# The inverse of an RWKV-7 chunk applied, transposed, to the increment's rows and the outputs' block instead of to the keys and the values

## The chip, the cores and the metric

One core of a Trainium2 chip. Five engines run their own queues: TensorE (PE, matrix products; its weight loads are listed apart as PEld), VectorE (DVE), ScalarE (ACT), GpSimd (POOL) and SyncE (SP, which here issues the DMA transfers). The metric is the device time of one execution in microseconds (us); lower is better. The kernel before took 3070.48 us, the median of three runs (3066.96 to 3072.09).

## The reference, cut to what matters

The kernel is one decoder block over 2048 positions of 1024 channels: normalise, one wide input projection, a convolution branch and an RWKV-7 branch, two output projections, a merge, a last projection, a residual and a norm. The change touches the RWKV-7 state alone:

```python
def _rwkv7_scan(r, decay, k, v, kk, b):
    def step(state, inp):
        r_t, w_t, k_t, v_t, kk_t, b_t = inp
        sk = jnp.einsum('bhvk,bhk->bhv', state, kk_t)
        state = (state * w_t[:, :, None, :] - sk[..., None] * b_t[:, :, None, :]
                 + v_t[..., None] * k_t[:, :, None, :])
        return state, jnp.einsum('bhvk,bhk->bhv', state, r_t)
```

There are 16 heads of 64 channels, and everything is fp32.

## The kernel before, in words

**Blocks, groups, chunks.** The sequence is cut into 4 blocks of 512 positions. In each block the 16 heads make 4 groups of 4 heads (2 pairs `q` of 2 heads `hh`), so there are 16 groups in all. In a group the scan runs over `NCH` = 8 chunks of 64 positions. Within a chunk the recurrence is a triangular system of 64 x 64 for each head; it is inverted ahead, and the state `S` is carried from chunk to chunk. Even chunks (`e` = 0) and odd chunks (`e` = 1) keep their blocks in opposite halves of the 128 partitions: `vrow(e)` is the lower half for `e` = 0 and the upper for `e` = 1, and `prow(e)` the other half.

**Preparation** (`pair`, L718). For each pair it makes scaled keys and receptances `KR`, scaled increments' keys `BK`, their masked products `As` (`aux<-KR,BK`), the transposed rows `tk` of `BK`, the decay `pe`, and the values' rows `uv`.

**The inverse** (`group`, L861). The 32 x 32 diagonal quarters of each triangular block go out by DMA, are inverted on POOL in a loop of 31 steps (`TT`, `itmp`), and come back into `As` (`As<-dT`).

**The prelude** (from L917). The rest of the inverse and its use are products on TensorE. `turns(lower)`: 32 products 32 x 32 for the off-diagonal quarter, with `T11`, the transposed upper diagonal quarter that DVE makes, into the banks `late` and `aux`; DVE copies them to `Qs`. `rows64(xv, values)`: 32 products 64 x 64 that apply the value block of `As` to `uv`, into two `xo` banks. `turns(upper)`: 32 products 32 x 32 that finish the quarter, copied back into `As`. Then the keys in `KR` are transposed (`pk`, 16 products, `xo<-ident,KR`), copied by ACT to `Kt`, multiplied by the inverse (`pw`, 32 products 64 x 64) and copied back to `KR`; and the inverse is applied to `uv` (`xu`, 32 products 64 x 64, copied back by DVE and ACT).

**The chunk loop** (L1022). For each chunk: the product of `KR` with the state (`xo<-S,KR`), `uv` plus it (DVE), the increment `tk` times `uv` into columns 2 and 3 of the chunk's `xo` bank, and four DVE operations that bring `S` forward from these columns (`S<-xo,pe,Se`). After each odd chunk the outputs of the two chunks are made: 8 products of `As` with `uv` into columns 0 and 1 of both `xo` banks (`xo<-uv,As`, 128 partitions, 64 columns), then copied by ACT.

**What sets the order.** Everything up to the last projections is written out in a planner's order: tasks are Python generators that yield the time from which they can go on; `note` (L85) books each instruction on its engine with a cost from a table and moves the planner's clock by TensorE's work; `poll` takes the tasks that are due. Between the steps of a group's chain the planner puts products of the input projection, three by three (`ps_main`, 128 x 128 by 512 columns). Each engine then runs its queue strictly in that order, and waits on semaphores. An fp32 product smaller than the whole array stands as two MATMUL records in the trace.

**Side work** (`sides`, L1316) runs beside it: the next block's norm, the convolution's layer norm of the block before (`lnorm_first`), and `presplit`, which splits the weights of the last projections into a high and a low part ahead of their use.

Of the kernel before, what the change touches and what calls it, by code (L numbers as in the profile page):

```python
# [9 lines left out]
F32 = mybir.dt.float32  # L10
# [8 lines left out]
P = 128  # L19
# [4 lines left out]
CH = 64  # L24
# [47 lines left out]
def hybrid_block(ctx: ExitStack, tc: tile.TileContext, x, vecs, convk, w2a2, final_g, ada, w_in, w_co, w_ro, w_o, crow, out,  # L72
# [12 lines left out]
    def note(name, op, out, ins):  # L85
# [9 lines left out]
        if name == "PE":  # L95
            if op == "transpose":
                part, c = False, 0.218
            else:
                K_, M_, N_ = ins[0].shape[0], size(ins[0]), size(ins[1])
                part = K_ <= 64 or M_ <= 64  # L100
                c = N_ / 600 * ((0.27 if K_ <= 64 else 0.54) if M_ <= 64 else 0.89 if part else 1.0)
                if ins[1].dtype == F32R:
                    part, c = False, 0.015 + N_ / 2400
            if part != kind[0]:
                kind[0], c = part, c + (0.1 if part else 0.24)
            now[0] = t + c
            end = now[0] + 0.2
            joined[0] = True
        elif name == "SP":
            vt["SP"] = t + 0.36  # L110
            vt["DMA"] = max(vt["DMA"], t) + size(out) * out.shape[0] * 4 / DMA_RATE
            end = vt["DMA"] + 1.9
        else:
            c0, c1_ = RATE[name] if op != "memset" else (0.1, 0.9e-3)
            end = vt[name] = t + c0 + c1_ * max([size(out)] + [size(a) for a in ins[:1]])
# [745 lines left out]
    def group(G, before):  # L861
# [52 lines left out]
        yield when(lambda: G.pairs == 2 and (before is None or before.chained))  # L914
        yield ok(*As)

        T11 = lt.tile([P, 2, 2, NCH // 2, 32], F32, name="T11", tag="i2")  # L917
        Qs = lt.tile([P, 2, 2, NCH // 2, 32], F32, name="Qs", tag="i2")

        def quarters(e):  # L920
            p0 = 64 - 64 * e
# [1 line left out]

        every = [(q, hh, c) for q in range(2) for hh in range(2) for c in range(NCH // 2)]

        for e in (1, 0):
            lo_, hi_ = quarters(e)
            for q in range(2):
                nc.vector.transpose(heads(T11[:, q])[lo_], heads(As[q])[lo_, e::2, lo_])
        yield both(ok(T11, uv), free, bank("late"), bank("aux", 2), bank("xo", 2))  # L930
        locked[0] = True
        chains[0] += 1
        pq = [p_.tile([P, 2, 2, NCH // 2, 32], F32, name=n_, tag=n_) for p_, n_ in ((pl, "late"), (pa, "aux"))]

        def turns(mul):
            for n, (q, hh, c) in enumerate(every[::-1]):
                for e in range(2):
                    mul(e, q, hh, c, dict(start=(n == 0), stop=(n == 15), skip_group_check=True))

        def lower(e, q, hh, c, kw):  # L940
            lo_, hi_ = quarters(e)
            nc.tensor.matmul(pq[e][hi_, q, hh, c, :], As[q][lo_, hh, 2 * c + e, hi_], T11[lo_, q, hh, c, :], **kw)

        def upper(e, q, hh, c, kw):
            lo_, hi_ = quarters(e)
            nc.tensor.matmul(pq[e][lo_, q, hh, c, :], Qs[hi_, q, hh, c, :], As[q][hi_, hh, 2 * c + e, hi_], **kw)

        O = uv[:, 0::2]
        Sg = S[g]

        def two():
            return [px.tile([P, 2, 2, P], F32, name="xo", tag="xo") for _ in range(2)]

        def rows64(bank_, mul):
            for turn in range(2):
                for cl in range(2):
                    for q in range(2):
                        for hh in range(2):
                            for e in range(2):
                                n_ = turn ^ e  # L960
                                mul(e, 2 * n_ + cl, q, hh, bank_[n_][prow(e), cl, q, 64 * hh:64 * hh + 64],
                                    dict(start=(cl + q + hh == 0), stop=(cl + q + hh == 3), skip_group_check=True))

        def keep64(bank_, half):
            for e in range(2):
                (nc.scalar.copy if e else nc.vector.tensor_copy)(uv[prow(e), 4 * half + e:4 * half + 4:2], bank_[half][prow(e)])

        def values(e, cc, q, hh, dst, kw):
            vr, c, hs = vrow(e), 2 * cc + e, slice(64 * hh, 64 * hh + 64)
            nc.tensor.matmul(dst, As[q][vr, hh, c, kcol(e)], uv[vr, c, q, hs], **kw)  # L970

        def solved(e, cc, q, hh, dst, kw):
            pr_, c, hs = prow(e), 2 * cc + e, slice(64 * hh, 64 * hh + 64)
            nc.tensor.matmul(dst, As[q][pr_, hh, c, kcol(e)], uv[pr_, c, q, hs], **kw)

        turns(lower)
        with tc.high_priority(HP):
            for e in (1, 0):
                lo_, hi_ = quarters(e)
                nc.vector.tensor_copy(Qs[hi_], pq[e][hi_])  # L980
        xv = two()
        rows64(xv, values)
        for half in range(2):
            keep64(xv, half)
        yield ok(Qs, uv)

        turns(upper)
        with tc.high_priority(HP):
            for e in range(2):
                lo_, hi_ = quarters(e)  # L990
                for q in range(2):
                    nc.vector.tensor_copy(As[q][lo_, :, e::2, hi_], pq[e][lo_, q])
        Kt = lt.tile([P, 2, NCH // 2, P], F32, name="Kt", tag="La", bufs=1)
        pk = [px.tile([P, NCH // 2, P], F32, name="xo", tag="xo") for _ in range(2)]
        for q in range(2):
            for cc in range(NCH // 2):
                for e in range(2):
                    nc.tensor.matmul(pk[q][prow(e), cc, :], R[q]["KR"][:, cc, CH * (1 + e):CH * (2 + e)], ident,
                                     start=(cc == 0), stop=(cc == NCH // 2 - 1), skip_group_check=True)
            nc.scalar.copy(Kt[:, q], pk[q])  # L1000
        yield ok(Kt, *As)

        pw = [p_.tile([P, 2, NCH // 2, CH], F32, name=n_, tag=n_) for p_, n_ in ((pl, "late"), (pa, "aux"))]
        for n, (q, hh, cc) in enumerate(every):
            hs = slice(64 * hh, 64 * hh + 64)
            for e in range(2):
                nc.tensor.matmul(pw[e][hs, q, cc, :], Kt[prow(e), q, cc, hs], As[q][prow(e), hh, 2 * cc + e, kcol(e)],
                                 start=(q + cc == 0), stop=(q == 1 and cc == NCH // 2 - 1), skip_group_check=True)
        with tc.high_priority(HP):
            for q in range(2):  # L1010
                for e in range(2):
                    nc.scalar.copy(R[q]["KR"][:, :, CH * (1 + e):CH * (2 + e)], pw[e][:, q])
        xu = two()
        rows64(xu, solved)
        for half in range(2):
            keep64(xu, half)
        locked[0] = False
        yield ok(uv, R[0]["KR"], R[1]["KR"])

        xo = [px.tile([P, 4, P], F32, name="xo", tag="xo") for _ in range(2)]  # L1020
        every = [(q, hh, slice(64 * hh, 64 * hh + 64)) for q in range(2) for hh in range(2)]
        for c in range(NCH):  # L1022
# [12 lines left out]
            if e == 0:  # L1035
                for q in range(2):
                    nc.tensor.matmul(b_[:, 2 + q, :], R[q]["tk"][:, c, :], uv[:, c, q, :], start=False, stop=(q == 1),
                                     skip_group_check=True)
            else:
                for q, hh, hs in every:  # L1040
                    nc.tensor.matmul(b_[hs, 2 + q, 0:64], R[q]["tk"][:, c, hs], uv[:, c, q, hs], start=False,
                                     stop=(q + hh == 2), skip_group_check=True)
            with tc.high_priority(HP):
                for q, hh, hs in every:
                    nc.vector.scalar_tensor_tensor(out=Sg[hs, q, hs], in0=b_[hs, 2 + q, slice(0, 64) if e else hs],
                                                   scalar=R[q]["pe"][hs, c:c + 1], in1=Se[hs, q, hs],
                                                   op0=ALU.mult, op1=ALU.add)
            if e:
                for n, (q, hh, hs) in enumerate(every):
                    for i in range(2):  # L1050
                        nc.tensor.matmul(xo[i][vrow(i), q, hs], As[q][:, hh, c - 1 + i, rcol(i)], uv[:, c - 1 + i, q, hs],
                                         start=False, stop=(n == 3), skip_group_check=True)
                with tc.high_priority(HP):
                    for i in range(2):
                        nc.scalar.copy(O[vrow(i), cc], xo[i][vrow(i), 0:2])
# [183 lines left out]
        hx.give(mean, rl)  # L1239

    def lora_split(ps, out_):
        yield hx.room(3)
        lf, ll, lx = hx.take("lora"), hx.take("lora_lo"), hx.take("lora_x")
        yield from shifted(ps, T_LORA, lambda: lf)
        Task(lora_parts(lf, ll, lx, out_), 0)

    def lora_parts(lf, ll, lx, out_):
        yield ok(lf)
        nc.scalar.activation(lf[0:64], lf[0:64], AF.Tanh)
        lw = e1.tile([P, TB], F32R, name="lw", tag="lw")  # L1250
        la = e1.tile([P, TB], F32R, name="la", tag="la")
# [64 lines left out]
    def sides(b, g):  # L1316
# [3 lines left out]
                normed[0] = b + 1  # L1320
        if b == 1 and g == 0:
            yield from gate_col()
        if b and g == 2:
            yield from lnorm_first(b - 1)
        if b in (1, 2):
            for _ in range((2, 2, 0, 4)[g]):
                n_ = later.pop(0)
                for half in range(2):
                    yield from presplit(*n_, half)
# [358 lines left out]
```

## Time and profile before

| | |
|---|---|
| median of three runs | 3070.48 us |
| the profiled execution | 3068.1 us |
| its span, first to last instruction | 3066.4 us |
| instructions | 53344 |
| TensorE busy | 2807.9 us |
| VectorE busy | 2029.4 us |
| ScalarE busy | 1111.8 us |
| GpSimd busy | 1264.2 us |
| mean granted TensorE clock | 0.979 |

A row of the groups' view names the line, the engine and the operation, the tile written and the tiles read, the shape as rows*columns of the array and what is streamed through, the count, then the busy time and the mean of one, and the idle time of the engine just before with what ended it. All instructions have the line of the recording helper, L129, so they are told apart by their tiles. A row of the timeline gives the start, the time from the first start to the last end, and how many like instructions were merged in it. Matmuls overlap in the array and their ends are modelled, so what one costs is read from starts: the start of the next minus its own.

### The profile page before, as it was taken

How to read it: one execution, taken by the hardware profiler on the slowest of the kernel's cores; microseconds unless marked ns; L12 is line 12 of the kernel's file. 1: busy time of each engine (PE TensorE's matmuls, PEld its weight loads, DVE VectorE, ACT ScalarE, POOL GpSimd, SP SyncE). 2: the span in 40 equal slices, each digit the busy share in tenths (PEclk: the TensorE clock that was granted, in tenths of full speed). 3: DMA queues.
4: the chain of work that ended last, by engine and by line, in shares of the span. 5: the costliest groups of instructions: out<-in, count | busy, mean ns of one | idle time of the engine just before them, and what ended most of it. 6: DMA issues, size and time to landing. Idle time of an engine off the chain costs nothing.

```text
span 3066.4 us, 53344 instructions
## 1 busy us (share of the span) xinstructions
PE 2807.9 (92%) x19984; PEld 2287.7 (75%) x19984; DVE 2029.4 (66%) x3525; ACT 1111.8 (36%) x2232; POOL 1264.2 (41%) x1762
## 2 busy tenths in 40 slices
PE   5999989999999999899999998999999988899998
PEld 4777777777777777677777776787777776788988
DVE  6786777877575868584767676757486846643433
ACT  4544444443243333433433344333333323321211
POOL 2564645442535555335347554354554614200000
PEclk9999999999999999999999998999999998899999
DMA  8775767766767667577567564775565856776665
GB/s 296 251 275 204 262 211 249 252 210 215 228 201 235 210 194 247 182 242 225 196 228 254 175 232 152 237 243 193 189 207 169 274 168 239 265 232 229 206 226 176
DMA packets 361746, 680.53 MB, mean 222 GB/s; under 512 B 134160, under 2 KB 152912, under 8 KB 361488
## 3 DMA queue, kind: packets, MB, share of 16 engines
q1 hardware_dynamic: 361488, 677.13, 66.0%
q8 instruction: 157, 2.57, 0.3%
q14 instruction: 101, 0.83, 0.1%
HBM read 494.34 MB, written 181.54 MB: 220 GB/s over the span
## 4 chain that ended last, share of the span: by engine, by line
PE 39%; DVE 9%; POOL 8%; DMA 7%; issue 3%; SPq 1%; ACT 1%; DVEq 0%; POOLq 0%; ACTq 0%
PE ps_main L129 25%; PE xo L129 5%; PE pout L129 5%; POOL TT L129 2%; PE aux L129 2%; POOL itmp L129 2%; DVE acc L129 2%; DVE S L129 2%; PE late L129 2%; SPq L129 1%; POOL lny L129 1%; DMA dn<-dN 1%; DMA zb<-bv_d 1%; POOL oc L129 1%; DMA w_st<-w_ro_t 1%
## 5 line engine op out<-in xcount | busy, mean ns | idle before, releaser
L129 PE MATMUL ps_main<-h_hi,w_hi 128*128 128x512 f32 x2432 | 1017.4, 418 | 24.0 <-ACT w_hi L129 9.4
L129 PE MATMUL ps_main<-h_hi,w_lo 128*128 128x512 f32 x2432 | 965.7, 397 | 11.7 <-DVE w_lo L129 5.0
L129 PE MATMUL ps_main<-h_lo,w_hi 128*128 128x512 f32 x2432 | 962.3, 396 | 1.0 <-DVE h_lo L129 1.0
L129 DVE SCALAR_TENSOR_TENSOR acc<-u,ck,acc 128x512 f32<-128x512 f32 x928 | 698.0, 752 | 28.5 <-POOL u L129 3.1
L129 PEld LDWEIGHTS ps_main<-h_hi,w_hi 128*128 128x128 f32 x2432 | 463.0, 190 | 139.0 <-issue 16.5
L129 PEld LDWEIGHTS ps_main<-h_hi,w_lo 128*128 128x128 f32 x2432 | 462.2, 190 | 122.2 <-DVE w_lo L129 7.4
L129 PEld LDWEIGHTS ps_main<-h_lo,w_hi 128*128 128x128 f32 x2432 | 463.9, 191 | 96.4 <-issue 8.4
L129 POOL TENSOR_TENSOR w_lo<-w_st,w_hi 128x1024 fp32r<-128x1024 f32 (+1 forms) x87 | 176.4, 2027 | 364.1 <-ACT w_hi L129 337.7
L129 POOL TENSOR_TENSOR TT<-TT,itmp 128x126 f32<-128x126 f32 (+22 forms) x496 | 206.4, 416 | 38.9
L129 ACT CAST w_hi<-w_st 128x1024 fp32r<-128x1024 f32 (+1 forms) x135 | 127.4, 944 | 256.2 <-DMA w_st<-w_co_t 156.4
L129 PE MATMUL xo<-uv,As 64*64 64x64 f32 (+1 forms) x3072 | 132.5, 226 | 94.6 <-DVE S L129 93.6
L129 POOL TENSOR_TENSOR itmp<-La,TT 128x126 f32<-128x126 f32 (+22 forms) x496 | 200.1, 403 | 43.2 <-issue 9.3
L129 ACT ACTIVATE th<-ps_main 128x512 f32<-128x512 f32 x160 | 95.7, 598 | 315.7 <-PE ps_main L129 248.5
L129 ACT COPY uv<-xo 64x256 f32<-64x256 f32 (+1 forms) x192 | 84.3, 439 | 343.8 <-PE xo L129 197.8
L129 DVE SCALAR_TENSOR_TENSOR S<-xo,pe,Se 64x64 f32<-64x64 f32 x512 | 145.0, 283 | 77.8 <-PE xo L129 61.5
L129 PEld LDWEIGHTS xo<-uv,As 64*64 64x64 f32 (+1 forms) x3072 | 113.6, 139 | 104.2 <-DVE S L129 102.4
L129 POOL TENSOR_TENSOR lny<-lny 128x512 f32<-128x512 f32 x90 | 119.9, 1340 | 117.7 <-DMA lny<-y_d 67.4
L129 ACT ACTIVATE Se<-S,pe 128x128 f32<-128x128 f32 x256 | 88.6, 394 | 131.2 <-DVE S L129 130.6
L129 DVE TENSOR_TENSOR uv<-xo,uv 64x256 f32<-64x256 f32 x128 | 54.0, 422 | 120.9 <-PE xo L129 118.1
L129 DVE TENSOR_TENSOR As<-aux,maskA 128x512 f32<-128x512 f32 x128 | 82.3, 685 | 62.3 <-PE aux L129 62.1
L129 DVE TENSOR_TENSOR w_lo<-w_st,w_hi 128x1024 fp32r<-128x1024 f32 x48 | 65.9, 1373 | 61.6 <-PE ps_main L129 45.8
L129 PEld LDWEIGHTS aux<-KR,BK 64*128 64x128 f32 x1024 | 65.7, 191 | 46.3 <-POOL KR L129 23.1
(292 smaller groups left out, 4921.3 us busy)
## 6 DMA issues: line engine op xcount, KB each, us to landing
w_hi<-kh_in SPq DMA_DIRECT2D x219, 512.0 KB
w_lo<-kl_in SPq DMA_DIRECT2D x219, 512.0 KB
w_st<-w_in_t SPq DMA_DIRECT2D x73, 512.0 KB
kh_in<-w_hi SPq DMA_DIRECT2D x71, 512.0 KB
kl_in<-w_lo SPq DMA_DIRECT2D x71, 512.0 KB
lny<-y_d SPq DMA_DIRECT2D x72, 256.0 KB
w_hi<-kh_ro SPq DMA_DIRECT2D x32, 512.0 KB
w_lo<-kl_ro SPq DMA_DIRECT2D x32, 512.0 KB
```

Source lines behind the costliest of these rows:

```text
L129: r = f(*a, **k)
```

## The change

The inverse, called `Tn` and kept transposed, is no longer applied to the keys and the values. It is applied to the increment's rows `tk` (`xo<-tk,Tn`) and to the output block of `As` (`late<-As,Tn`, `aux<-As,Tn`), 64 products 64 x 64; `KR` is left as it is, and its transposes, `Kt` and the copies go. The 32 products 32 x 32 of the lower quarter and the 32 products 64 x 64 of the values are issued in turns, one and one, each in the half of the partitions that the other doesn't use. In the chunk loop the outputs of two chunks directly follow the odd chunk's increment, ahead of the state's update. `Tn` has 64 columns, a right half that POOL sets to zero, and four more DVE transposes. The planner's cost for products of at most 64 columns is one number instead of two. `lora_split` takes its buffers later, `lnorm_first` moves from the third group of a block to the second, and half of the `presplit` work moves to the last block.

```diff
-                c = N_ / 600 * ((0.27 if K_ <= 64 else 0.54) if M_ <= 64 else 0.89 if part else 1.0)
+                c = N_ / 600 * (0.55 if M_ <= 64 else 0.89 if part else 1.0)
...
-        T11 = lt.tile([P, 2, 2, NCH // 2, 32], F32, name="T11", tag="i2")
+        Tn = lt.tile([P, 2, 2, NCH // 2, CH], F32, name="Tn", tag="La", bufs=1)
...
+        nc.gpsimd.memset(Tn[:, :, :, :, right], 0.0)
+        for b_, col in ((0, left), (1, right)):
+            for e in (1, 0):
+                sl = quarters(e)[b_]
+                for q in range(2):
+                    nc.vector.transpose(heads(Tn[:, q])[sl, :, col], heads(As[q])[sl, e::2, sl])
...
+                for n in range(32):
+                    e, (q, hh, c) = n % 2, every[n // 2]
+                    lo_, hi_ = quarters(e)
+                    nc.tensor.matmul(pq[e][hi_, q, hh, c, :], As[q][lo_, hh, 2 * c + e, hi_], Tn[lo_, q, hh, c, left],
+                                     start=(n < 2), stop=(n >= 30), skip_group_check=True)
+                    h_, m = (n // 16) ^ e, n // 2 % 8
+                    cl, q, hh = m // 4, m // 2 % 2, m % 2
+                    vr, cv, hs = vrow(e), 4 * h_ + 2 * cl + e, slice(64 * hh, 64 * hh + 64)
+                    nc.tensor.matmul(xv[h_][prow(e), cl, q, hs], As[q][vr, hh, cv, kcol(e)], uv[vr, cv, q, hs],
+                                     start=(m == 0), stop=(m == 7), skip_group_check=True)
...
+                for e in range(2):
+                    for half in range(2):
+                        nc.scalar.copy(uv[prow(e), 4 * half + e:4 * half + 4:2], xv[half][prow(e)])
...
-        turns(lower)
...
-        rows64(xv, values)
...
-                    nc.tensor.matmul(pk[q][prow(e), cc, :], R[q]["KR"][:, cc, CH * (1 + e):CH * (2 + e)], ident,
...
-                nc.tensor.matmul(pw[e][hs, q, cc, :], Kt[prow(e), q, cc, hs], As[q][prow(e), hh, 2 * cc + e, kcol(e)],
...
-        rows64(xu, solved)
...
+        for turn in range(2):
+            for n in range(16):
+                e, cc, hh = n % 2, n // 2 % 4, n // 8
+                q, pr_, hs = turn ^ e, prow(e), slice(64 * hh, 64 * hh + 64)
+                for out_, rhs in ((py[q][pr_, cc, hs], tk[q][pr_, 2 * cc + e, hs]),
+                                  (pg[q][pr_, hh, cc, :], As[q][pr_, hh, 2 * cc + e, rcol(e)])):
+                    nc.tensor.matmul(out_, Tn[pr_, q, hh, cc, :], rhs, start=(n < 2), stop=(n >= 14), skip_group_check=True)
+        with tc.high_priority(HP):
+            for e in range(2):
+                for q, cp in enumerate((nc.scalar.copy, nc.vector.tensor_copy)):
+                    cp(tk[q][prow(e), e::2, :], py[q][prow(e)])
+            for e in range(2):
+                for q, cp in enumerate((nc.scalar.copy, nc.vector.tensor_copy)):
+                    cp(As[q][prow(e), :, e::2, rcol(e)], pg[q][prow(e)])
...
+            if e:
+                for n, (q, hh, hs) in enumerate(every):
+                    for i in range(2):
+                        nc.tensor.matmul(xo[i][vrow(i), q, hs], As[q][:, hh, c - 1 + i, rcol(i)], uv[:, c - 1 + i, q, hs],
+                                         start=False, stop=(n == 3), skip_group_check=True)
             with tc.high_priority(HP):
                 for q, hh, hs in every:
                     nc.vector.scalar_tensor_tensor(out=Sg[hs, q, hs], in0=b_[hs, 2 + q, slice(0, 64) if e else hs],
...
             if e:
-                for n, (q, hh, hs) in enumerate(every):
-                    for i in range(2):
-                        nc.tensor.matmul(xo[i][vrow(i), q, hs], As[q][:, hh, c - 1 + i, rcol(i)], uv[:, c - 1 + i, q, hs],
-                                         start=False, stop=(n == 3), skip_group_check=True)
...
-        if b and g == 2:
+        if b and g == 1:
             yield from lnorm_first(b - 1)
-        if b in (1, 2):
-            for _ in range((2, 2, 0, 4)[g]):
+        if b:
+            for _ in range((4, 2, 2, 0)[g] if b + 1 == NB else (1, 0, 1, 2)[g]):
```

The new order at two places. First TensorE's queue in the first group's prelude, where the lower quarter's products end and the values' begin. A row is a product: the tile written, the tiles read (`T11` or `Tn` the transposed quarter, `As` the blocks of one pair, `uv` the values), and the size of what it writes. Before, the last two of the 32 small products, then all 32 values' products as one run, then the projection:

```order
L129 MATMUL late<-T_2159,As 32x32
L129 MATMUL aux<-T_2159,As 32x32
L129 MATMUL xo<-uv,As 64x64 x32
L129 MATMUL ps_main<-h_hi,w_hi 128x512
L129 MATMUL ps_main<-h_lo,w_hi 128x512
L129 MATMUL ps_main<-h_hi,w_lo 128x512
```

Now, with the buffers' numbers (`As_781` and `As_782` are the two pairs, `xo_2270` and `xo_2271` the two banks):

```order
L129 MATMUL late_2268<-Tn_2159,As_781 32x32
L129 MATMUL xo_2270<-uv_779,As_782 64x64
L129 MATMUL aux_2269<-Tn_2159,As_781 32x32
L129 MATMUL xo_2271<-uv_779,As_782 64x64
L129 MATMUL late_2268<-Tn_2159,As_782 32x32
L129 MATMUL xo_2271<-uv_779,As_781 64x64
L129 MATMUL aux_2269<-Tn_2159,As_782 32x32
L129 MATMUL xo_2270<-uv_779,As_781 64x64
```

The same 64 products now alternate between 32 x 32 and 64 x 64 from the first to the last: 63 changes of the array's tiling in a prelude where there was one.

Second, TensorE's queue at an odd chunk in the first group's loop, with the engines whose semaphores each row waits for. Before:

```order
L129 MATMUL xo<-uv,tk 64x64 [waits DVE_49]
L129 MATMUL xo<-uv,tk 64x64 x3
L129 MATMUL xo<-uv,As 64x64
L129 MATMUL xo<-uv,As 64x64 [waits DVE_49]
L129 MATMUL xo<-uv,As 64x64 x6
L129 MATMUL ps_main<-h_hi,w_hi 128x512
```

Now:

```order
L129 MATMUL xo<-uv,tk 64x64 [waits DVE_49]
L129 MATMUL xo<-uv,tk 64x64 x3
L129 MATMUL xo<-uv,As 64x64 x8
L129 MATMUL ps_main<-h_hi,w_hi 128x512
L129 MATMUL ps_main<-h_lo,w_hi 128x512
```

The second output product no longer waits for DVE, and the eight stand as one run. Behind them come six products of the projection in both kernels, then the next even chunk's product with the state. Before, the last three of the six and that product:

```order
L129 MATMUL ps_main<-h_hi,w_hi 128x512
L129 MATMUL ps_main<-h_lo,w_hi 128x512
L129 MATMUL ps_main<-h_hi,w_lo 128x512
L129 MATMUL xo<-S_437,KR 128x128 [waits Activation_49]
L129 MATMUL xo<-S_437,KR 128x128
```

Now:

```order
L129 MATMUL ps_main<-h_hi,w_hi 128x512
L129 MATMUL ps_main<-h_lo,w_hi 128x512
L129 MATMUL ps_main<-h_hi,w_lo 128x512
L129 MATMUL xo<-S_437,KR 128x128 [waits DVE_49,Activation_49]
L129 MATMUL xo<-S_437,KR 128x128 [waits DVE_49]
```

The wait for DVE has moved from the second output product to this one. DVE's first update of an odd chunk waits for a semaphore that the last of the eight output products raises; before, the last product of the increment raised it.

More of the change, by code (lines that the diff above doesn't have):

```diff
@@ L915, in group @@
         yield ok(*As)
-        T11 = lt.tile([P, 2, 2, NCH // 2, 32], F32, name="T11", tag="i2")
+        Tn = lt.tile([P, 2, 2, NCH // 2, CH], F32, name="Tn", tag="La", bufs=1)
         Qs = lt.tile([P, 2, 2, NCH // 2, 32], F32, name="Qs", tag="i2")
+        tk = [r_["tk"] for r_ in R]
+        left, right = slice(0, 32), slice(32, 64)
         def quarters(e):
@@ L924, in group @@
         every = [(q, hh, c) for q in range(2) for hh in range(2) for c in range(NCH // 2)]
[L926 to L933, printed above, removed]
@@ L935, in turns @@
-        def turns(mul):
-            for n, (q, hh, c) in enumerate(every[::-1]):
-                for e in range(2):
[L938 to L946, printed above, removed]
+        nc.gpsimd.memset(Tn[:, :, :, :, right], 0.0)
@@ new lines, in group @@
+        for b_, col in ((0, left), (1, right)):
[3 more added lines that the diff above has]
+                    nc.vector.transpose(heads(Tn[:, q])[sl, :, col], heads(As[q])[sl, e::2, sl])
+            if b_ == 0:
+                yield both(ok(Tn, uv), free, bank("late"), bank("aux", 2), bank("xo", 2))
+                locked[0] = True
+                chains[0] += 1
+                pq = [p_.tile([P, 2, 2, NCH // 2, 32], F32, name=n_, tag=n_) for p_, n_ in ((pl, "late"), (pa, "aux"))]
+                xv = [px.tile([P, 2, 2, P], F32, name="xo", tag="xo") for _ in range(2)]
+                for n in range(32):
[9 more added lines that the diff above has]
+                with tc.high_priority(HP):
+                    for e in (1, 0):
+                        hi_ = quarters(e)[1]
+                        nc.vector.tensor_copy(Qs[hi_], pq[e][hi_])
+                for e in range(2):
+                    for half in range(2):
+                        nc.scalar.copy(uv[prow(e), 4 * half + e:4 * half + 4:2], xv[half][prow(e)])
@@ new lines, in group @@
+        yield ok(Qs, Tn)
+        for n, (q, hh, c) in enumerate(every):
+            for e in range(2):
+                hi_ = quarters(e)[1]
+                nc.tensor.matmul(pq[e][hi_, q, hh, c, :], As[q][hi_, hh, 2 * c + e, hi_], Qs[hi_, q, hh, c, :],
+                                 start=(n == 0), stop=(n == 15), skip_group_check=True)
+        with tc.high_priority(HP):
+            for e in (1, 0):
+                hi_ = quarters(e)[1]
+                nc.vector.tensor_copy(Tn[hi_, :, :, :, left], pq[e][hi_])
@@ new lines, in group @@
+        yield both(ok(Tn, uv), bank("xo", 2))
+        py = [px.tile([P, NCH // 2, P], F32, name="xo", tag="xo") for _ in range(2)]
+        pg = [p_.tile([P, 2, NCH // 2, CH], F32, name=n_, tag=n_) for p_, n_ in ((pl, "late"), (pa, "aux"))]
+        for turn in range(2):
[5 more added lines that the diff above has]
+                    nc.tensor.matmul(out_, Tn[pr_, q, hh, cc, :], rhs, start=(n < 2), stop=(n >= 14), skip_group_check=True)
@@ L948, in group @@
+        with tc.high_priority(HP):
+            for e in range(2):
[4 more added lines that the diff above has]
+                    cp(As[q][prow(e), :, e::2, rcol(e)], pg[q][prow(e)])
+        locked[0] = False
         O = uv[:, 0::2]
         Sg = S[g]
-        def two():
-            return [px.tile([P, 2, 2, P], F32, name="xo", tag="xo") for _ in range(2)]
@@ L954, in rows64 @@
[L954 to L974, printed above, removed]
@@ L976, in group @@
-        turns(lower)
[L977 to L981, printed above, removed]
-        rows64(xv, values)
[L983 to L997, printed above, removed]
-                    nc.tensor.matmul(pk[q][prow(e), cc, :], R[q]["KR"][:, cc, CH * (1 + e):CH * (2 + e)], ident,
-                                     start=(cc == 0), stop=(cc == NCH // 2 - 1), skip_group_check=True)
-            nc.scalar.copy(Kt[:, q], pk[q])
@@ L1001, in group @@
[L1001 to L1006, printed above, removed]
-                nc.tensor.matmul(pw[e][hs, q, cc, :], Kt[prow(e), q, cc, hs], As[q][prow(e), hh, 2 * cc + e, kcol(e)],
-                                 start=(q + cc == 0), stop=(q == 1 and cc == NCH // 2 - 1), skip_group_check=True)
@@ L1009, in group @@
[L1009 to L1013, printed above, removed]
-        rows64(xu, solved)
[L1015 to L1018, printed above, removed]
+        yield ok(*tk)
         xo = [px.tile([P, 4, P], F32, name="xo", tag="xo") for _ in range(2)]
@@ L1241, in lora_split, with lora_parts @@
     def lora_split(ps, out_):
-        yield hx.room(3)
-        lf, ll, lx = hx.take("lora"), hx.take("lora_lo"), hx.take("lora_x")
+        yield hx.room(1)
+        lf = hx.take("lora")
         yield from shifted(ps, T_LORA, lambda: lf)
-        Task(lora_parts(lf, ll, lx, out_), 0)
-    def lora_parts(lf, ll, lx, out_):
-        yield ok(lf)
+        Task(lora_parts(lf, out_), 0)
+    def lora_parts(lf, out_):
+        yield both(ok(lf), hx.room(2))
+        ll, lx = hx.take("lora_lo"), hx.take("lora_x")
         nc.scalar.activation(lf[0:64], lf[0:64], AF.Tanh)
```

## The prediction

> **What bounds the kernel now.** I read the page first: busy shares by engine, and the 40 slices.
>
> ```profile
> PE 2807.9 (92%) x19984; PEld 2287.7 (75%) x19984; DVE 2029.4 (66%) x3525; ACT 1111.8 (36%) x2232; POOL 1264.2 (41%) x1762
> PE   5999989999999999899999998999999988899998
> DVE  6786777877575868584767676757486846643433
> ```
>
> TensorE is at nine tenths in nearly every slice and DVE at seven to eight, so in each stage time is what TensorE's queue takes, waits included. Then the table of waits for PE (engine and tile that waited, who released it, total, times, longest):
>
> ```profile
> PE xo L129 <- DVE S L129: 94.8, 65, 3.5
> ...
> PE aux L129 <- POOL KR L129: 15.1, 14, 3.6
> PE late L129 <- DVE T L129: 13.8, 5, 6.0
> ...
> PE aux L129 <- DVE As L129: 10.4, 6, 4.0
> ```
>
> One wait towers over the rest. The groups by form say which products it is:
>
> ```profile
> L129 PE MATMUL xo<-S,KR 128*128 128x128 f32 x512 | 83.6, 286 | 1.5 <-DVE S L129 1.3
> ...
> L129 PE MATMUL xo<-uv,As 128*64 128x64 f32 x1024 | 62.2, 231 | 93.6 <-DVE S L129 93.6
> ```
>
> The outputs of two chunks (128*64) lose 93.6 us; the products with the state, which need the same update for their data, lose 1.3. The timeline of the first group's first two chunks shows how:
>
> ```profile
> 231.27 0.71 PE L129 MATMUL xo<-uv,tk 128*128 128x128 f32 x4
> ...
> 232.09 1.21 DVE L129 SCALAR_TENSOR_TENSOR S<-xo,pe,Se 64x64 f32<-64x64 f32 x4 [0.87 <-PE xo L129]
> ...
> 233.21 0.64 PE L129 MATMUL xo<-S,KR 128*128 128x128 f32 x4
> ...
> 234.59 0.45 PE L129 MATMUL xo<-uv,tk 128*64 128x64 f32 x8 [0.31 <-DVE uv L129]
> 234.88 0.28 PE L129 MATMUL xo<-uv,As 128*64 128x64 f32 x2
> 235.16 1.23 DVE L129 SCALAR_TENSOR_TENSOR S<-xo,pe,Se 64x64 f32<-64x64 f32 x4 [0.62 <-PE xo L129]
> 236.43 0.76 DVE L129 SCALAR_TENSOR_TENSOR acc<-u,ck,acc 128x512 f32<-128x512 f32 x1
> 236.45 0.68 PE L129 MATMUL xo<-uv,As 128*64 128x64 f32 x14 [1.29 <-DVE S L129]
> 237.06 0.50 PE L129 MATMUL ps_main<-h_hi,w_hi 128*128 128x512 f32 x1
> ```
>
> After the even chunk, TensorE does projection products from the increment at 231.27 to 233.21 while DVE updates the state. After the odd chunk it starts the outputs at once; the first (two records) goes to the other bank, the second writes the bank that DVE reads, and the whole queue stands from 235.16 to 236.45. So often: 64 pairs of chunks in 16 groups x 4.
>
> **The change, part by part.** All sums are against the profiled execution's 3068.1 us (span 3066.4), which lies 2.4 under the median shown.
>
> *The outputs ahead of the update.* The wait of 93.6 us goes. What is late next is the update: it now starts behind eight products more, 236.45 to 237.06, some 0.6 us; then 1.23 us of DVE, while TensorE has six projection products. Even chunks run that cover today (six products up to 233.21) and lose 1.3 us in all. From the last output's start the update takes about 0.28 + 1.23 us (234.88 to 235.16 is the lag that the row shows), the six products 6 x 0.23 = 1.4: short by 0.1 us at worst for the second half of the state. I take -92; bounds -94 and -35 (the rival on this below).
>
> *Keys left as they are.* The rows around the transposes in the first prelude:
>
> ```profile
> 221.70 0.19 PE L129 MATMUL aux<-As,Qs 32*32 32x32 f32 x1
> 221.82 0.44 PE L129 MATMUL xo<-ident,KR 128*64 128x128 f32 x4
> ...
> 223.72 0.50 PE L129 MATMUL ps_main<-h_hi,w_hi 128*128 128x512 f32 x1
> ...
> 224.62 0.27 PE L129 MATMUL late<-As,Kt 64*64 64x64 f32 x1
> ...
> 225.90 0.27 PE L129 MATMUL xo<-uv,As 64*64 64x64 f32 x1
> ...
> 226.01 2.03 PE L129 MATMUL xo<-uv,As 64*64 64x64 f32 x63
> 227.97 0.50 PE L129 MATMUL ps_main<-h_hi,w_hi 128*128 128x512 f32 x1
> ```
>
> From the last small product to the projection: 223.72 - 221.70 = 2.02 us, of which the step from a small product back to the full array stays (0.12, below). Saved 1.9 x 16 = -30 us. It is TensorE's own time, so nothing hides it.
>
> *64 products with the inverse instead of 64.* Before: 227.97 - 224.62 = 3.35 us, the keys' 32 in 1.28, the values' 32 in 2.07. The new ones use two tiles of the array, as the values' products do: 2 x 1.92 + 0.15 = 4.0, so +0.65 x 16 = +10. Bounds: at the keys' pace 2.7, -10; if two in a row on one tile lose the overlap of the tiles (216.41 to 218.28 is 0.03 for each of 64 records, below, four of them 0.12 a product) 7.7 us, +70. I take +10, the row of the same tiles.
>
> *Two kinds of product in turns.* This is the large term. The rows at the borders of today's runs:
>
> ```profile
> 215.28 0.21 PE L129 MATMUL late<-T,As 32*32 32x32 f32 x1
> ...
> 215.34 0.19 PE L129 MATMUL late<-T,As 32*32 32x32 f32 x1
> ...
> 216.29 0.19 PE L129 MATMUL aux<-T,As 32*32 32x32 f32 x1
> 216.41 2.08 PE L129 MATMUL xo<-uv,As 64*64 64x64 f32 x64
> ...
> 218.28 0.22 PE L129 MATMUL xo<-uv,As 64*64 64x64 f32 x1
> 218.43 0.50 PE L129 MATMUL ps_main<-h_hi,w_hi 128*128 128x512 f32 x1
> ```
>
> Inside a run products on different tiles overlap: 64 records 32 x 32 start within 1.0 us, 64 records 64 x 64 within 1.9. Where the form changes, nothing overlaps: the first 64 x 64 starts 0.12 us after the last 32 x 32, and the first full product 0.15 after the last 64 x 64. [...] If each change costs that, a product also pays its own two records one after the other: 0.055 for the small one (215.28 to 215.34), 0.11 for the large (225.90 to 226.01). A pair is 0.055 + 0.12 + 0.11 + 0.15 = 0.43 us, 32 pairs 13.8 us. Both runs take 218.43 - 215.28 = 3.15 today. So +10.6 us x 16 groups = +170. Bounds: in the trace all changes of form have partitions in common, and in the new order neighbours use opposite halves; if halves are independent the changes cost nothing, and the smaller products vanish under the larger (2.1 us instead of 3.15): -17.
>
> [...]
>
> *DVE, ACT, POOL.* DVE loses the copies of values and of the quarter and gains transposes and copies:
>
> ```profile
> L129 DVE COPY uv<-xo 64x512 f32<-64x512 f32 x64 | 41.7, 691 | 77.6 <-PE xo L129 77.6
> L129 DVE STREAM_TRANSPOSE T<-As 32x256 f32<-32x256 f32 x64 | 25.5, 420 | 32.2 <-DMA As<-dT 31.8
> L129 DVE COPY As<-late 32x256 f32<-32x256 f32 x32 | 12.2, 417 | 21.2 <-PE aux L129 21.2
> ...
> L129 DVE COPY Qs<-aux 32x512 f32<-32x512 f32 x16 | 10.9, 684 | 32.1 <-PE aux L129 30.5 <-POOL lny L129 1.6
> ```
>
> Out: 41.7 + 2 x 12.2. In: 64 transposes of 0.42, 32 copies like `Qs` of 0.69, 64 copies of 0.69: 27 + 22 + 44. Net +27 us on an engine idle for a third; ACT changes by less. TensorE's projection products between the steps hide it; without that cover it would be 27 / 16 = 1.7 us a group. I count 0. Queued behind a DVE or ACT copy that waits for a slow prelude are convolution taps and evacuations, which TensorE needs later by as much as it is itself late.
>
> *Planner's cost, side work.* The planner now books (32 + 64) / 600 x 0.55 = 0.09 us for a pair of alternating products; if they take 0.43, TensorE arrives some 11 us later at each group's next steps than planned, and waits for POOL and DVE (15.1 + 13.8 + 10.4 = 39.3 above) shrink: -10, between 0 and -39. The moved side work keeps its number of operations and runs on POOL, ACT and DMA; its shift between blocks I count at 0, +-5.
>
> Sum: -92 - 30 + 10 + 170 - 10 = +48; 3068.1 + 48 = 3116, and 3118 beside the median.
>
> **The rivals.** *Halves are independent, changes drain only within a half.* Then a product waits for the one two places back that used its half: 0.11 + 0.15 = 0.26 us a pair, 8.3 us, +5.2 x 16 = +83 instead of +170. Sum -39: 3031, faster. For it: overlap between tiles within a run. Against: the large products at 216.41 follow small ones on both halves, which a drain by halves and a drain of all explain alike, so the rows don't decide. [...]
>
> *No drain at all between halves.* The term is -17 to 0, say -8; no late arrival, so the -10 goes: -92 - 30 + 10 - 8 = -120, 2950. For it: nothing in the trace tests opposite halves. Against: unlike forms never overlap in it.
>
> *The wait only moves.* The price of the drain as forecast, and the state's update not covered: it decides where a convolution tap (0.76 us, 236.43) stands in DVE's queue ahead of the update. Then 0.76 + 0.1 of 64 waits come back, +55: 3173. Against: even chunks carry taps too and lose 1.3.
>
> **How the numbers follow.** Full drain 0.60 (3118; its own range 3085 to 3150: 0.38 to 0.47 us a pair is -26 to +20, the late arrivals -29 to +10, and both at one end is unlikely); drain by halves 0.14; no drain 0.16; the wait moves 0.10. About 0.04 of the first falls below 3070 (a pair at 0.33 us or less). Faster by over 0.2% (6 us, what a measurement of this kernel tells from none): 0.14 + 0.16 + 0.04 = 0.34; within 0.03; slower 0.63. The range 3015 to 3160 takes in the halves and leaves out no drain and half of the moved wait.
>
> **What would show it.** The prelude's 64 alternating products take near 13.8 us from the first `late<-Tn,As` to the next `ps_main` (8.3 or 2 to 3 by the rivals). The row `xo<-uv,As` 128*64 has no idle time for DVE, and `xo<-S,KR` stays at a few us (over 50 by the third). `xo<-ident,KR` is gone; the 64 `Tn` products take about 4 us a group. I am wrong if the prelude is short, or if a wait on POOL or DMA of 50 us or more stands in the table of waits.

## The result, and the profile after

The changed kernel takes 3224.57 us, the median of four runs (3219.16 to 3230.24), against 3071.28 us for the kernel before (the median of four, one run more than in the table above): a ratio of 1.049, 95% interval 1.045 to 1.053. It is slower, as forecast, but by 153 us and not by 48, and the range (3015 to 3160) doesn't hold it.

The page of the changed kernel: busy shares, then TensorE's busy tenths and its granted clock in 40 slices.

```profile
span 3220.6 us, 52325 instructions
PE 3038.3 (94%) x19472; PEld 2433.9 (76%) x19472; DVE 2040.9 (63%) x3556; ACT 1105.0 (34%) x2200; POOL 1269.6 (39%) x1779
PE   5999999989899999999999999999999999799998
PEclk9989898979989899899998998998898989899999
```

512 TensorE records fewer, and 230 us more of busy TensorE. The mean granted clock of the whole run fell from 0.979 to 0.936. The groups by form show where the time is:

```profile
L129 PE MATMUL xo<-uv,As 64*64 64x64 f32 x1024 | 224.7, 317 | 0.0
L129 PE MATMUL xo<-S,KR 128*128 128x128 f32 x512 | 82.1, 281 | 1.4 <-ACT rh L129 1.1
...
L129 PE MATMUL aux<-Tn,As 32*32 32x32 f32 x512 | 75.2, 236 | 0.0
L129 PE MATMUL late<-Tn,As 32*32 32x32 f32 x512 | 74.7, 234 | 8.8 <-DVE Tn L129 8.8
...
L129 PE MATMUL xo<-uv,As 128*64 128x64 f32 x1024 | 40.8, 222 | 0.0
```

The last row is the success: the outputs (128*64) have no idle time ahead of them, where 93.6 us stood, and the products with the state wait for DVE no more than before. The other rows are the loss: 1024 records of the values cost 224.7 us of busy time, where 2048 cost 70.2; the small products cost 75.2 and 74.7, where each had 20.5.

The timeline of TensorE in the first group's prelude, at its beginning and where it ends:

```profile
219.87 0.24 PE L129 MATMUL late<-Tn,As 32*32 32x32 f32 x2
220.04 0.32 PE L129 MATMUL xo<-uv,As 64*64 64x64 f32 x2
220.30 0.24 PE L129 MATMUL aux<-Tn,As 32*32 32x32 f32 x2
220.47 0.33 PE L129 MATMUL xo<-uv,As 64*64 64x64 f32 x2
...
236.68 0.31 PE L129 MATMUL late<-Tn,As 32*32 32x32 f32 x2
236.91 0.47 PE L129 MATMUL xo<-uv,As 64*64 64x64 f32 x2
237.31 0.31 PE L129 MATMUL aux<-Tn,As 32*32 32x32 f32 x2
237.55 0.47 PE L129 MATMUL xo<-uv,As 64*64 64x64 f32 x2
237.96 0.79 PE L129 MATMUL ps_main<-h_hi,w_hi 128*128 128x512 f32 x1
238.55 0.63 PE L129 MATMUL ps_main<-h_lo,w_hi 128*128 128x512 f32 x1
238.97 0.63 PE L129 MATMUL ps_main<-h_hi,w_lo 128*128 128x512 f32 x1
...
241.91 0.40 PE L129 MATMUL ps_main<-h_hi,w_hi 128*128 128x512 f32 x1
```

The first pair takes 220.30 - 219.87 = 0.43 us, exactly the price of the prediction. The last takes 237.31 - 236.68 = 0.63. And the projection products behind it, which need 0.23 us each at full clock, take 0.43 until 241.5. The same stretch by windows: the window, its length, the busy time of PE, PEld, DVE, ACT and POOL, the granted clock, the DMA share and GB/s:

```profile
200.00:219.80 19.80, 17.80 (x99) 13.66 (x97) 16.37 (x28) 9.71 (x19) 12.40 (x11) 0.91 0.84 283
219.80:225.00 5.20, 5.20 (x49) 3.90 (x48) 0.00 (x0) 0.00 (x0) 0.00 (x0) 0.98 0.19 54
225.00:238.00 13.00, 13.00 (x83) 9.24 (x82) 0.34 (x1) 0.00 (x0) 0.00 (x0) 0.50 0.00 0
238.00:242.00 4.00, 4.00 (x11) 3.18 (x11) 3.33 (x7) 2.13 (x4) 0.00 (x0) 0.52 0.02 4
242.00:262.00 20.00, 20.00 (x287) 16.77 (x286) 11.26 (x22) 9.44 (x21) 4.78 (x2) 1.00 0.56 198
```

From 225 to 238 TensorE is listed as busy for all 13.00 us, and its granted clock is 0.50. The clock is full at the start of the prelude, halves 4.9 us into it, and comes back 3.9 us after it. DVE, ACT, POOL and the DMA stand still meanwhile: the prelude is a hole in the whole program. From the first small product to the next projection product the sixteen preludes take 17.7 to 20.5 us each, 303 us in all, where the two runs of the kernel before took 54 (14 of its preludes 3.14 us, and two, at half clock, 4.9 and 5.3).

### The profile page after: what moved, and what is told of

Its sections match the earlier page's. It is cut to its first block, busy times and chain, and to the rows that moved or that the text cites. A ratio compares the mean times of both kernels' runs of the same rounds, so it can differ in the third digit from the quotient of the medians.

```text
span 3220.6 us, 52325 instructions
## 1 busy us (share of the span) xinstructions
PE 3038.3 (94%) x19472; PEld 2433.9 (76%) x19472; DVE 2040.9 (63%) x3556; ACT 1105.0 (34%) x2200; POOL 1269.6 (39%) x1779
## 5 line engine op out<-in xcount | busy, mean ns | idle before, releaser
L129 PE MATMUL xo<-uv,As 128*64 128x64 f32 (+1 forms) x2048 | 265.5, 269 | 0.0
L129 DVE COPY Qs<-aux 32x512 f32<-32x512 f32 x16 | 10.9, 683 | 305.2 <-PE aux L129 305.2
L129 PEld LDWEIGHTS xo<-uv,As 128*64 128x64 f32 (+1 forms) x2048 | 169.7, 161 | 29.9
L129 PE MATMUL aux<-KR,BK 64*128 64x128 f32 x1024 | 81.9, 293 | 24.8 <-POOL KR L129 15.2
```

Of the source, the lines that this page charges most:

```text
L129: r = f(*a, **k)
```

## The experiments

**The two kinds as two runs.** In the changed kernel, the small products first, then the values':

```diff
-                for n in range(32):
+                for kind_, n in [(k_, i_) for b0_ in range(0, 32, 32) for k_ in range(2) for i_ in range(b0_, b0_ + 32)]:
                     e, (q, hh, c) = n % 2, every[n // 2]
-                    lo_, hi_ = quarters(e)
-                    nc.tensor.matmul(pq[e][hi_, q, hh, c, :], ...)
+                    if kind_ == 0:
+                        lo_, hi_ = quarters(e)
+                        nc.tensor.matmul(pq[e][hi_, q, hh, c, :], ...)
+                        continue
```

> The changed kernel, with the 32 small products (32 x 32) first and the 32 values' products (64 x 64) behind them, as two runs. Theory 1 (each change of tiling drains the array, and an array kept draining falls to half clock): the two kinds took 303 us of TensorE in the changed kernel against 53 before, and the projection products 33 us more; both come back, 3224 - 250 - 33 = about 2940 us, 4% under the kernel before, and no granted clock under 0.97. Rival (the loss is in the rest of the change, the longer chain of transposes and copies and the moved side work): over 3010 us.

Measured: 2941.99 us, ratio to the kernel before 0.957 (0.954 to 0.960). Its timeline and windows at the same prelude:

```profile
217.42 0.19 PE L129 MATMUL aux<-Tn,As 32*32 32x32 f32 x1
217.54 2.08 PE L129 MATMUL xo<-uv,As 64*64 64x64 f32 x64
219.55 0.51 PE L129 MATMUL ps_main<-h_hi,w_hi 128*128 128x512 f32 x1
219.89 0.40 PE L129 MATMUL ps_main<-h_lo,w_hi 128*128 128x512 f32 x1
```

```profile
216.40:219.60 3.20, 3.20 (x130) 3.09 (x129) 1.90 (x4) 0.00 (x0) 0.00 (x0) 1.00 0.32 86
219.60:236.00 16.40, 16.40 (x248) 13.86 (x247) 8.42 (x16) 8.33 (x15) 3.31 (x2) 1.00 0.42 140
```

The prelude's first part is 3.2 us long and the clock stays at 1.00; so it does in 14 of the 16 preludes, and two are at half clock, as in the kernel before. The order of these 64 products alone costs 3225 - 2942 = 283 us. The rest of the change is a gain of 4.3%, and this kernel is faster than both.

**The turns put into the kernel before**, and nothing else:

```diff
-        turns(lower)
+        xv = two()
+        for n in range(32):
+            e, (q, hh, c) = n % 2, every[n // 2]
+            lower(e, q, hh, c, dict(start=(n < 2), stop=(n >= 30), skip_group_check=True))
+            h_, m = (n // 16) ^ e, n // 2 % 8
+            cl, q, hh = m // 4, m // 2 % 2, m % 2
+            values(e, 2 * h_ + cl, q, hh, xv[h_][prow(e), cl, q, 64 * hh:64 * hh + 64], ...)
...
-        xv = two()
-        rows64(xv, values)
```

> The kernel before, with only this of the change: small products and values' products in turns, one and one. Theory 1: 3071 + 250 + 33 = about 3350 us, granted clock near 0.94. Rival A (drain without the clock): 3071 + 170 = 3240. Rival B (turns cost nothing by themselves): 3071.

Measured: 3363.71 us, ratio 1.094 (1.091 to 1.098), granted clock 0.933. The same loss, 289 us over the 3074.47 us that the kernel before took beside it, in a kernel that shares nothing else with the change. Both rivals of the expectation fall: 3240 us, the changes' price without the half clock, and 3071, turns that cost nothing by themselves.

**The turns cut into pieces**, with projection products between; `after` makes the planner go on with other tasks:

```diff
...
+                    if kind_ == 1 and n % 4 == 3 and n < 31:
+                        yield after(1.3)
```

> The changed kernel, with the alternating products cut into 8 pieces of 4 pairs, and projection products (128 x 128 by 512) between the pieces: as many changes between the two kinds, but never more than 2 us of them at a stretch. Theory 1 (0.43 us a pair at full clock, and half clock only after some us of an emptied array): pairs stay at 0.43 us, 16 x 13.8 = 220 us instead of 303; with 7 more entries and exits a group (some 0.1 us each, +11) and no slow projection products (-33): about 3120 us. Rival (a change of tiling costs by itself what the changed kernel shows, 0.6 us a pair, and the low clock is only a reading): 3200 us or more.

Measured: 3159.77 us, granted clock 0.971. A piece in its timeline:

```profile
219.63 0.24 PE L129 MATMUL late<-Tn,As 32*32 32x32 f32 x2
219.80 0.33 PE L129 MATMUL xo<-uv,As 64*64 64x64 f32 x2
220.06 0.24 PE L129 MATMUL aux<-Tn,As 32*32 32x32 f32 x2
...
221.34 0.50 PE L129 MATMUL ps_main<-h_hi,w_hi 128*128 128x512 f32 x1
221.68 0.39 PE L129 MATMUL ps_main<-h_lo,w_hi 128*128 128x512 f32 x1
221.91 0.39 PE L129 MATMUL ps_main<-h_hi,w_lo 128*128 128x512 f32 x1
```

The same products with the same changes between them take 0.43 us a pair (220.06 - 219.63), and the products behind them 0.23. So a pair costs 0.43 at full clock, and the 0.63 of the changed kernel comes with a long stretch of such pairs. The total lies between the two numbers expected, and 40 us over theory 1's: an entry costs 0.1 us (0.33 to the first small product instead of 0.23) and so does the first projection product behind a piece (221.68 - 221.34 = 0.34), so seven more entries and exits are 7 x 0.2 x 16 = 22 us and not 11. The other 30 are half clock that the pieces did not avoid: 57 of the 512 pairs took 0.64 us (57 x 0.21 = 12), and 181 projection products started at half clock, where the kernel of two runs has 92 (89 x 0.2 = 18).

**Both products of a pair reading the same half** of the partitions, instead of opposite halves:

```diff
...
+                    e = 1 - n % 2
                     h_, m = (n // 16) ^ e, n // 2 % 8
...
```

> The changed kernel with the values' product of each pair taken from the same half of the partitions as the small product before it, and not from the other. Theory 1 (a change of tiling empties the whole array, wherever the products lie): 3224, within 15 us. Rival (opposite halves overlap in part, and that is already in the 3224): slower by 50 us or more.

Measured: 3222.53 us, ratio 1.048 (1.044 to 1.052), granted clock 0.935. Its first pair:

```profile
218.92 0.24 PE L129 MATMUL late<-Tn,As 32*32 32x32 f32 x2
219.10 0.33 PE L129 MATMUL xo<-uv,As 64*64 64x64 f32 x2
219.35 0.24 PE L129 MATMUL aux<-Tn,As 32*32 32x32 f32 x2
```

The edit does less than its name says, and "the half of the partitions that the other doesn't use" above holds for reading alone. A small product reads and writes the half `prow(e)`; a values' product reads `vrow(e)` and writes `prow(e)`. So in the changed kernel the two products of a pair read opposite halves but write the same one, and a values' product and the small product behind it read the same half and write opposite ones. The edit exchanges the two cases. No two neighbours share both, in either kernel, and the steps are the same: 0.17 to 0.18 us from a small product to a large one, 0.25 to 0.26 from a large one to a small one. Neither a common half to read nor a common half to write decides the price, and the prediction's rivals of independent halves are wrong. Neighbours of unlike form that share neither half were not run.

**Turns of eight, and of two.** The loop of the first experiment with blocks of 8 and of 2 instead of 32: 7 and 31 changes instead of 63.

```diff
-                for kind_, n in [... for b0_ in range(0, 32, 32) ... range(b0_, b0_ + 32)]:
+                for kind_, n in [... for b0_ in range(0, 32, 8) ... range(b0_, b0_ + 8)]:
```

> The changed kernel with small and values' products in turns of eight and eight: 7 changes of tiling in a prelude instead of 63, where the kernel in two runs (2942 us) has 1. Theory 1: 6 changes more, each 0.12 to 0.15 us plus the unhidden first load of some 0.05, so 6 x 0.19 = 1.1 us a group, 18 us in all, at full clock: 2960 us. Rival (any alternation at all brings the half clock, 3 us a prelude and more): 3000 us or more.

> The changed kernel with small and values' products in turns of two and two: 31 changes of tiling in a prelude, each turn on both halves. At full clock a turn of two takes as long as a turn of one, 0.055 + 0.12 + 0.11 + 0.15 = 0.43 us for four products, so 16 x 0.43 = 7 us a prelude, +3.8 over the two runs' 3.15, 62 us in all: 2942 + 62 = 3004 us if the clock stays full. If the array, emptied as often per us as in turns of one, falls to half clock after 4 to 8 us, part of the last 3 us of each prelude and some 8 projection products behind it (0.2 us each) cost more, up to 3 us a group: 3050. Theory 1 expects the second, 3020 to 3050, and a granted clock of 0.95 to 0.97.

Measured: 2954.01 us (ratio 0.962, 0.960 to 0.963), granted clock 0.981, and 3053.42 us (0.994, 0.992 to 0.996), granted clock 0.960. The windows of the first prelude in turns of two:

```profile
219.00:223.00 4.00, 4.00 (x76) 3.02 (x72) 0.00 (x0) 0.00 (x0) 0.00 (x0) 0.98 0.25 70
223.00:228.00 5.00, 5.00 (x58) 3.68 (x55) 0.93 (x2) 0.54 (x2) 0.00 (x0) 0.50 0.00 0
```

Half as many changes still bring the half clock: the time is 49 us over the 3004 forecast for full clock, and 3 over the upper end of theory 1. Turns of eight don't bring it: 14 of the 16 preludes take 3.93 us at full clock, 0.13 us for each of the six changes more where the forecast had 0.19 (its 0.05 for a first load was an estimate that no run shows), and two are at half clock, as in the kernel of two runs. Fewer changes also make a shorter prelude (3.9 us, where turns of two take 7.5 to 10.5 and turns of one 17.7 to 20.5), so these runs don't settle whether their number or the length of the stretch matters; for the number speaks that in the changed kernel the halving had come within 3.9 us in 10 of the 16 preludes.

**The outputs' place.** Behind the update again in the kernel of two runs (the edit shown), and ahead of it in the kernel before (the reverse):

```diff
-            if e:
-                for n, (q, hh, hs) in enumerate(every):
-                    for i in range(2):
-                        nc.tensor.matmul(xo[i][vrow(i), q, hs], ...)
             with tc.high_priority(HP):
                 for q, hh, hs in every:
                     nc.vector.scalar_tensor_tensor(out=Sg[hs, q, hs], ...)
+            if e:
+                for n, (q, hh, hs) in enumerate(every):
+                    for i in range(2):
+                        nc.tensor.matmul(xo[i][vrow(i), q, hs], ...)
```

> The kernel in two runs (2942 us), with the outputs of two chunks put back behind the state's update. Theory 1: the wait for DVE returns at the second output product, 94 us of idle TensorE and 115 us of its time at these products: 3036 to 3057 us. Rival (the order of the outputs is worth little, since the wait only moves to the next product with the state): 2942 to 2960.

> The kernel before, with only the outputs put ahead of the state's update. Theory 1: the same 94 to 115 us: 2960 to 2980 us. Rival: 3060 to 3075.

Measured: 3043.56 us (ratio 0.991, 0.990 to 0.993) and 2967.89 us (0.967, 0.965 to 0.969). The groups with the outputs behind the update, then with the outputs ahead in the kernel before:

```profile
L129 PE MATMUL xo<-S,KR 128*128 128x128 f32 x512 | 82.0, 281 | 3.7 <-DVE S L129 3.2
L129 PE MATMUL xo<-uv,As 128*64 128x64 f32 x1024 | 61.3, 228 | 88.4 <-DVE S L129 88.4
```

```profile
L129 PE MATMUL xo<-S,KR 128*128 128x128 f32 x512 | 82.2, 280 | 3.1 <-DVE S L129 2.4
...
L129 PE MATMUL xo<-uv,As 128*64 128x64 f32 x1024 | 40.8, 222 | 0.0
```

The wait comes and goes with the place of eight products, and doesn't reappear at the product with the state (3.1 us idle in all). It is worth 102 and 104 us, more than the 93.6 us of idle: the outputs' own busy time falls from 62.2 to 40.8 as well, since they run as one burst.

**The planner's cost and the side work** in the kernel before, together with `lora_split`, and then the planner's cost alone:

```diff
-                c = N_ / 600 * ((0.27 if K_ <= 64 else 0.54) if M_ <= 64 else 0.89 if part else 1.0)
+                c = N_ / 600 * (0.55 if M_ <= 64 else 0.89 if part else 1.0)
```

> The kernel before, with only the planner's cost for narrow products, the later buffers of lora_split and the moved side work of the change. Forecast: within 15 us of 3071. Rival (the planner's truer cost is itself worth something): 3050 or less.

> The kernel before with only the planner's cost for narrow products. With the side work as well it took 3054 us. If the planner's truer cost gives the 17 us: 3050 to 3060. If the moved side work and the later buffers do: 3066 to 3076.

Measured: 3054.45 us (ratio 0.994, 0.993 to 0.996) for all of it, 2 us outside the 15 that were forecast, and 3074.93 us (1.000, 0.998 to 1.002) for the cost alone. So the moved side work and the later buffers, with the new cost, are worth 17 us, and the cost by itself nothing that can be told. The two were not separated further; in the profile the gain is spread over small waits (`late` on the transposes from 13.8 to 6.0 us, `ps_main` on `mr` from 12.5 to 6.0).

## Why the prediction was wrong

The sign, the price of each change at full clock and the place were right; the largest term of the sum was too small, because the halved clock that the changes bring (0.50 in the trace after) stood in no term.

- *Two kinds of product in turns: +170 forecast, +283 measured* (3225 against 2942; +289 in the kernel before). This is the step that failed. The step priced a pair by the borders of runs in the trace of before, 0.43 us, and the trace after shows 0.43 for the first pairs. What it left out is that every one of those borders had been measured at full clock, and that 32 such pairs in a row don't keep it. The profiles of the changed kernel and of the kernel of two runs split the term. The preludes take 303 us against 55: 32 x 16 pairs of 0.43 would have been 220, so 220 - 55 = 165 is the price of the changes at full clock, near the 170 forecast, and 303 - 220 = 83 is the half clock (388 of the 512 pairs take 0.64 us). The projection products, each taken to the next start on TensorE without idle time, fill 2069 us against 2039: 31 more, all with those that start at half clock. 165 + 83 + 31 = 279 of the 287 between the two profiled executions; 5 of the rest are idle time.
- *The price does not go by halves.* Forecast at 0.60, with 0.14 for a price by halves and 0.16 for none. The prediction said that neighbours in the new order use opposite halves; that is so of what they read or of what they write, never of both. The first pairs of the changed kernel at 0.43 us, and 3222.5 us against 3224.6 with the halves exchanged, decide against the two rivals: the steps at a change are 0.17 and 0.26 us in the changed kernel, 0.18 and 0.25 with the halves exchanged. The overlap within a run on which the first rival rested (64 records 32 x 32 start within 1.0 us) did not appear at a change of form. That the array drains at a change was the prediction's reading of such steps: the runs show when the next product starts, not what it waits for.
- *The outputs ahead of the update: -92 forecast, -104 and -102 measured.* The wait did not move to the next product (`xo<-S,KR`, 1.4 us idle): the cover of six projection products holds after odd chunks too, as the prediction had read it from the even ones. The third rival is wrong.
- *Keys left as they are, and 64 products instead of 64: -30 + 10 forecast, -11 measured*, as the difference of two kernels (3043.6 with the outputs behind the update, 3054.5 without the new products). The products themselves were sized right: the 64 take 64.7 us in 16 groups by starts, 4.0 a group as forecast, and two in a row on one tile cost nothing more. The difference of the two kernels also holds the longer chain of DVE copies and transposes, which the prediction counted at 0. In their profiles TensorE's own time (starts, idle time left out) falls by 28 us and its idle time grows by 20, spread over many waits (`pmean` on POOL from 2.9 to 12.3, `ps_main` on `mr` from 6.0 to 13.1, nearly all of both from 2570 us on).
- *Side work: 0 +-5 forecast, -17 measured.* *Fewer waits on POOL and DVE: -10 forecast;* the three rows went from 39.3 to 32.9 us.

The measured parts, -104 - 11 - 17 + 283 = +151, make the 153 that was measured. This sum is no test by itself: with -102 for the first, the four are the steps of one chain of kernels from before to after, which must add up. What tests the parts is that the outputs and the turns were each worth nearly the same alone in the kernel before (104 against 102, 289 against 283).

## What to carry to other kernels

Keep TensorE products of one tiling together: a change between 32 x 32 and 64 x 64 cost 0.12 to 0.15 us at full clock, whether the neighbours shared the half that they read or the half that they write, and turns of eight cost 12 us in this kernel where turns of one cost 283. A price read at single borders was a price at full clock here; before multiplying it by thirty, ask whether the stretch that it makes still keeps the clock (here 388 of 512 pairs took 0.64 us and not 0.43), and count the full-size work behind it that pays too (31 us here). And look at who shares a PSUM bank with an update: moving eight products ahead of the reader that held their bank took 102 and 104 us in the two kernels where it was tried, out of 3071.

## What the runs showed of the hardware that was not expected

TensorE can be listed as busy all the time and still run at half clock: 13.00 us busy of 13.00 at a granted clock of 0.50 (225 to 238 us of the changed kernel). The ends of products are modelled in the profile, so "busy" says only that the next one followed without a listed gap. The halving came 1.4 to 5.7 us into the alternating products in 14 preludes (0.2 us in another, and in one it was there from the start), full-size products behind it ran at 0.43 instead of 0.23 us until the clock came back, 2.7 to 5.6 us behind the prelude, and 1.7 us pieces with 1.6 us of full-size products between them mostly kept the full clock (455 of 512 pairs). The traces of the kernel before and of the changed one show no granted clock but 0.5 and 1.0, and each of their 54 and 66 stretches at one level, but for the last of each trace, lasts a whole multiple of 3.41 us: in the first prelude of the changed kernel the half clock lasts from 224.78 to 241.85, 17.07 us. So the clock halves here in a stretch for which the profile lists no idle time; what the halving follows, the number of the changes or how little the small products use the array, was not measured.
